# A DeltaNet and latent-attention trunk on one core: how layer A issues its small TensorE products

## The chip, the core and the metric

The kernel runs on one core of a Trainium2 chip. The time is device microseconds of one execution; three runs of the kernel before took 1349.76, 1353.17 and 1352.13, a median of 1352.13. The engines are TensorE (PE, with its weight load PEld), VectorE (DVE), ScalarE (ACT), GpSimd (POOL) and SyncE (SP), which issues the DMAs.

## The reference

A trunk of two layers over 1024 tokens of width 1024, with 16 learned meta tokens ahead of them. Layer A is a gated DeltaNet with 8 heads of 128: queries, keys and values from one projection, a causal convolution over four tokens and Silu, then the gated delta rule. Then a key and value set for latent attention is built, and layer B reads it. The change is in layer A alone:

```
qkv = silu(causal_dwconv(z[..., :2 * DN_KW + DN_VW], conv_w))
q = l2_norm(q) * (DN_DK ** -0.5);  k = l2_norm(k)
beta = sigmoid(b_raw);  g = -exp(a_log) * softplus(a_raw + dt_bias)
S_t = a_t S_{t-1} (I - b_t k_t k_t^T) + b_t v_t k_t^T,  o_t = S_t q_t      # a = exp(g)
o = rms_norm(o, o_gain) * silu(gate);  x + o @ w_out
```

The reference does the rule in chunks of tokens: inside a chunk a lower triangular system has to be solved, and a 128x128 state S goes from chunk to chunk.

## The kernel before, in words

Tokens are cut into a meta tile of 16 and eight tiles of 128. The normed input lies transposed in SBUF as two tensors hT_hi and hT_lo (reduced-precision parts that add up to the fp32 value). A projection of 128 columns is a `gemm_T` (L207) for each of three token chunks of 272, 384 and 384: 8 x 3 products called *split products* here (L91, L92, L93: high x high, high x low, low x high), accumulated in one of two "mm" banks of PSUM. ScalarE copies the result out (L370), POOL and DVE do the convolution (L372, and L375 three times), ScalarE the Silu.

The heads go in pairs. For a pair: the keys, then `key_prep` for both heads, `invert_blocks`, the values and their transposes (`natural`), the queries, `query_prep`, `finish_inverses`, and the scan over the tiles (`scan_meta`, then `scan_tile` eight times for each head). While one pair is at its inverse and scan, the projections of the next pair's keys are already issued; these split products are the work that fills PE between the small ones.

`key_prep` transposes the keys tile by tile (L397); after each, ScalarE squares the transposed tile and adds up its rows. It forms beta over the key's norm (br), which is transposed too (L416, L417), copied and written to DRAM as rows (L420, L421), makes the decay tile from two products (L431), the key products (L440) and the meta tile's (L449, L454). U goes to DRAM as 32x32 blocks (blk_in). `invert_blocks` loads these as M, 66 blocks side by side, and bb, the beta row read from DRAM (L516); after the product of the two (L519) come 31 steps of two DVE operations each (L524, L527) that hang on one another. A POOL operation (L529) follows and the store to blk_out. `finish_inverses` loads the blocks back as T64, transposes them on DVE (L554), and joins them to 64 and 128 rows with small products on PE (from L566 on, "fin" bank).

`query_prep` squares the whole of qT on ScalarE, then sums over the 128 rows of each tile with a product whose moving side is one column of ones (L475); then the products of queries and keys (L483, and L487 for the meta tile). A scan step is: S times keys (L611), r on DVE, S times queries (L615), the inverse times r (L616), u on DVE, u into the state (L621), S2 on DVE, u into the output (L625).

PSUM has two "mm" banks, three "tr", one "fin" and two "ch" for the scan. What sets the order on each engine is the scheduler of the framework: it takes the program as written and places each instruction where its model has it ready; PE, DVE, ACT, POOL and SP each run their list in that order. An instruction that waits holds up all that is behind it on its engine. After layer A's scan come the output norms (L693 on POOL), the gates, and the split of the output weights.

Of the kernel before, what the change touches and what calls it, by code (L numbers as in the profile page):

```python
# [16 lines left out]
F32 = mybir.dt.float32  # L17
# [13 lines left out]
H = 8  # L31
# [85 lines left out]
def body(ctx: ExitStack, tc: tile.TileContext, I, out):  # L117
# [64 lines left out]
    with ExitStack() as la:  # L182
# [78 lines left out]
        with ExitStack() as l0:  # L261
# [5 lines left out]
            wab2 = ap_.tile([P, KT, 2, 2 * H], F32R, tag="wab2", name="wab2", bufs=1)  # L267
            split_w(wab, wab2[:, :, 0], wab2[:, :, 1])
            abT = ap_.tile([4 * H, L], F32, tag="abT", name="abT", bufs=1)
            for c, (a, b) in enumerate(TOKC):  # L270
                ps = bank("fin", [P, 512])[0:4 * H, 0:b - a]
                for kt in range(KT):
                    w = wab2[:, kt].rearrange("p x c -> p (x c)")
                    TE.matmul(ps, w, hT_hi[:, kt, a:b], start=kt == 0, stop=False)
                    TE.matmul(ps, w, hT_lo[:, kt, a:b], start=False, stop=kt == KT - 1)
                V.tensor_copy(abT[:, a:b], ps)
            ab = ap_.tile([P, NT + 1, 2 * H], F32, tag="ab", name="ab", bufs=1)
            V.memset(ab, 0.0)
            ps = bank("tr", [P, 512])
            for t in range(-1, NT):  # L280
                a, b = tok(t)
                s = t if t >= 0 else NT
                TE.transpose(ps[0:b - a, 32 * s:32 * s + 32], abT[:, a:b], ident[:32, :32])
            for rows, s in ((slice(0, P), slice(0, NT)), (slice(0, NM), slice(NT, NT + 1))):
                p4 = ps[rows, 32 * s.start:32 * s.stop].rearrange("p (t x c) -> p t x c", x=2, c=2 * H)
                V.tensor_copy(ab[rows, s], p4[:, :, 0])
                V.tensor_tensor(out=ab[rows, s], in0=p4[:, :, 1], in1=ab[rows, s], op=ALU.add)
# [32 lines left out]
            V.tensor_tensor(out=glo, in0=g, in1=ghi, op=ALU.subtract)  # L320

# [61 lines left out]
        def key_prep(h, kn, U):  # L383

            att, kd = ([kp.tile([P, 4, P], F32, tag=y, name=nm(y), bufs=6) for _ in range(2)] for y in ("att", "kd"))
            kdm = sp.tile([NM, P], F32, tag="kdm", name=nm("kdm"), bufs=3)
# [4 lines left out]
            for half, s4 in halves() + [(2, slice(NT, NT + 1))]:  # L391
                k, tiles = (P, range(s4.start, s4.stop)) if half < 2 else (NM, (-1,))
                ps = bank("tr", [P, 4, P])
                junk = sp.tile([P, P], BF16, tag="jk", name=nm("junk"), bufs=1)
                for j, t in enumerate(tiles):
                    a, b = tok(t)
                    TE.transpose(ps[0:k, j, :], kn[:, a:b], ident)  # L397
                    act(junk[0:k], ps[0:k, j, :], AF.Square, accum_out=sk[0:k, s4.start + j, hc])
                rk4, sc4 = flat(rk[0:k, s4, hc]), sc[0:k, s4]
                rsqrt(rk4, flat(sk[0:k, s4, hc]), 1.0, EPS)  # L400
                V.tensor_tensor(out=sc4, in0=rk4, in1=flat(ekd[0:k, s4, hc]), op=ALU.mult)
                if half < 2:
                    V.tensor_tensor(out=kd[half], in0=ps, in1=sc4[:, :, None].broadcast_to([P, 4, P]),
                                    op=ALU.mult)
                else:
                    V.tensor_scalar(out=kdm, in0=ps[0:k, 0, :], scalar1=sc4, scalar2=None, op0=ALU.mult)
            for rows, s in ((slice(0, P), slice(0, NT)), (slice(0, NM), slice(NT, NT + 1))):
                x = lambda y: flat(y[rows, s, hc])
                V.tensor_tensor(out=x(br), in0=x(beta), in1=x(rk), op=ALU.mult)
                V.tensor_scalar(out=x(nbeta), in0=x(br), scalar1=-1.0, scalar2=None, op0=ALU.mult)  # L410
                if s.start == 0:
# [1058 lines left out]
```

## Time and profile before

| what | value |
|---|---|
| median of three runs | 1352.13 us (1349.76 to 1353.17) |
| the profiled execution | 1351.8 us, span 1350.1 us |
| mean granted TensorE clock | 0.989 |
| PE busy | 1306.3 us, 97% of the span |
| DVE busy | 900.1 us, 67% |
| ACT busy | 534.8 us, 40% |
| POOL busy | 412.8 us, 31% |
| last product of layer A's scan | ends at 572.8 us (572.41 + 0.43) |

The profile shows one execution. In a group's line stand source line, engine, operation, "out<-in" by the program's names, how often, then busy us and the mean ns of one, and behind the bar the idle time before them and what ended it. In a timeline stand the start, the time, the engine and the line, and in square brackets an idle time before it. A product of two fp32 operands shows as two records (x2). PE's records overlap, so the cost of one is read from the distance between starts.

### The profile page before, as it was taken

How to read it: one execution, taken by the hardware profiler on the slowest of the kernel's cores; microseconds unless marked ns; L12 is line 12 of the kernel's file. 1: busy time of each engine (PE TensorE's matmuls, PEld its weight loads, DVE VectorE, ACT ScalarE, POOL GpSimd, SP SyncE). 2: the span in 40 equal slices, each digit the busy share in tenths (PEclk: the TensorE clock that was granted, in tenths of full speed). 3: DMA queues.
4: the chain of work that ended last, by engine and by line, in shares of the span. 5: the costliest groups of instructions: out<-in, count | busy, mean ns of one | idle time of the engine just before them, and what ended most of it. 6: DMA issues, size and time to landing. Idle time of an engine off the chain costs nothing.

```text
span 1350.1 us, 24895 instructions
## 1 busy us (share of the span) xinstructions
PE 1306.3 (97%) x9064; PEld 1181.7 (88%) x9064; DVE 900.1 (67%) x2601; ACT 534.8 (40%) x1694; POOL 412.8 (31%) x680
## 2 busy tenths in 40 slices
PE   6999999999999999999999999998999999998998
PEld 4879989989998999997888798887999999998876
DVE  6669879968978884633553765224888878788221
ACT  6442343244325322211222243116777677776100
POOL 3344224323421320060101402212535435347000
PEclk9999999999999999999999999999999999999999
DMA  6111202111211113255441302311111101014443
GB/s 185 41 25 48 56 20 62 40 42 37 59 49 32 50 32 96 72 159 178 145 147 68 95 1 84 121 47 57 44 38 35 56 21 36 21 36 149 133 124 125
DMA packets 116924, 96.81 MB, mean 72 GB/s; under 512 B 28462, under 2 KB 106094, under 8 KB 116802
## 3 DMA queue, kind: packets, MB, share of 16 engines
q1 hardware_dynamic: 116802, 95.23, 23.7%
q8 instruction: 71, 1.16, 0.4%
q14 instruction: 51, 0.42, 0.1%
HBM read 68.19 MB, written 27.01 MB: 71 GB/s over the span
## 4 chain that ended last, share of the span: by engine, by line
PE 75%; DVE 8%; DMA 5%; POOL 5%; ACT 4%; issue 3%; SPq 0%; DVEq 0%; ACTq 0%; POOLq 0%
PE mm L91 7%; PE mm L93 7%; PE mm L92 7%; PE sc L93 6%; PE sc L92 6%; PE sc L91 6%; PE bd L91 3%; PE bd L93 3%; PE bd L92 3%; PE pt L1312 2%; PE tr L483 1%; DMA raw<-in_a_w_out 1%; ACT junk L82 1%; DMA out<-raw 1%; PE ch L625 1%
## 5 line engine op out<-in xcount | busy, mean ns | idle before, releaser
L91 PE MATMUL mm<-hT_hi,whi 128*128 128x384 f32 (+1 forms) x768 | 256.8, 334 | 3.5 <-DVE whi L98 3.5
L93 PE MATMUL mm<-hT_hi,wlo 128*128 128x384 f32 (+1 forms) x768 | 255.3, 332 | 0.7 <-DVE wlo L99 0.7
L92 PE MATMUL mm<-hT_lo,whi 128*128 128x384 f32 (+1 forms) x768 | 255.7, 333 | 0.0
L91 PEld LDWEIGHTS mm<-hT_hi,whi 128*128 128x128 f32 x768 | 147.4, 192 | 5.5 <-issue 4.7
L93 PEld LDWEIGHTS mm<-hT_hi,wlo 128*128 128x128 f32 x768 | 147.5, 192 | 2.5 <-DVE wlo L99 1.3
L92 PEld LDWEIGHTS mm<-hT_lo,whi 128*128 128x128 f32 x768 | 147.2, 192 | 1.4 <-issue 0.4
L108 DVE TENSOR_TENSOR pTl<-pt,pTh 128x256 fp32r<-128x256 f32 (+2 forms) x112 | 55.0, 494 | 11.0 <-ACT pTh L107 9.5
L98 POOL TENSOR_SCALAR whi<-raw 128x512 fp32r<-128x512 f32 x48 | 37.7, 799 | 70.4 <-PE mm L92 63.8
L82 ACT ACTIVATE P<-P,mx 128x144 f32<-128x144 f32 (+3 forms) x64 | 50.6, 791 | 21.8 <-DVE mx L1270 19.0
L91 PE MATMUL sc<-wo_hi,oTh 128*128 128x512 f32 (+1 forms) x144 | 57.5, 400 | 0.6 <-issue 0.6
L93 PE MATMUL sc<-wo_hi,oTl 128*128 128x512 f32 (+1 forms) x144 | 57.2, 397 | 0.0
L92 PE MATMUL sc<-wo_lo,oTh 128*128 128x512 f32 (+1 forms) x144 | 56.9, 395 | 0.0
L375 DVE SCALAR_TENSOR_TENSOR kn<-z,pcol,kn 128x384 f32<-128x384 f32 (+1 forms) x72 | 41.4, 576 | 19.4 <-POOL kn L372 18.8
L1283 POOL TENSOR_SCALAR P<-P,sl 128x144 f32<-128x144 f32 (+3 forms) x64 | 53.0, 829 | 3.7
L370 ACT COPY z<-mm 128x384 f32<-128x384 f32 (+1 forms) x72 | 31.8, 442 | 54.4 <-PE mm L93 54.3
L107 ACT CAST pTh<-pt 128x256 fp32r<-128x256 f32 (+2 forms) x112 | 47.3, 427 | 14.1 <-PE pt L1312 8.0
L99 DVE TENSOR_TENSOR wlo<-raw,whi 128x512 fp32r<-128x512 f32 x64 | 47.1, 746 | 8.5 <-POOL whi L98 8.4
L93 PE MATMUL sc<-h_hi,wlo 128*128 128x512 f32 x128 | 50.8, 397 | 0.0
L92 PE MATMUL sc<-h_lo,whi 128*128 128x512 f32 x128 | 50.6, 396 | 0.0
L91 PE MATMUL sc<-h_hi,whi 128*128 128x512 f32 x128 | 50.5, 395 | 0.0
L91 PE MATMUL bd<-wf_hi,oTh 128*128 128x512 f32 x128 | 50.2, 392 | 0.3 <-ACT oTh L1422 0.2
L102 DVE SCALAR_TENSOR_TENSOR wlo<-raw,pcol,whi 128x128 fp32r<-128x128 f32 x64 | 23.4, 429 | 40.0 <-POOL whi L101 40.0
(380 smaller groups left out, 3951.1 us busy)
## 6 DMA issues: line engine op xcount, KB each, us to landing
raw<-in_a_w_in SPq DMA_DIRECT2D x64, 256.0 KB
xt<-in_x SPq DMA_DIRECT2D x16, 512.0 KB
o_scr<-o SPq DMA_DIRECT2D x64, 64.0 KB
raw<-in_a_w_out SPq DMA_DIRECT2D x8, 512.0 KB
on<-o_scr SPq DMA_DIRECT2D x8, 512.0 KB
x_scr<-xt SPq DMA_DIRECT2D x8, 512.0 KB
raw<-in_b_w_in SPq DMA_DIRECT2D x8, 512.0 KB
gb_scr<-z SPq DMA_DIRECT2D x8, 512.0 KB
```

Source lines behind the costliest of these rows:

```text
L82: i = A.activation(out_ap, in_ap, func, **kw)
L91: TE.matmul(ps, ahi, bhi, start=first, stop=False)
L92: TE.matmul(ps, ahi, blo, start=False, stop=False)
L93: TE.matmul(ps, alo, bhi, start=False, stop=last)
L98: eng.tensor_scalar(out=hi, in0=raw, scalar1=1.0, scalar2=1.0, op0=ALU.mult, op1=ALU.mult)
L99: V.tensor_tensor(out=lo, in0=raw, in1=hi, op=ALU.subtract)
L107: A.copy(hi, ps)
L108: V.tensor_tensor(out=lo, in0=ps, in1=hi, op=ALU.subtract)
L370: A.copy(z[:, 3 + a:3 + b], gemm_T(hi, lo, c))
L375: V.scalar_tensor_tensor(out=yc, in0=z[:, a + j:b + j], scalar=col("cw", 24 * j + m), in1=yc, op0=ALU.mult, op1=ALU.add)
L1283: G.tensor_scalar(out=Pm[:, 0:n], in0=Pm[:, 0:n], scalar1=s, scalar2=1.0, op0=ALU.mult, op1=ALU.mult)
L1312: TE.transpose(pt[:, kb, x * P:(x + 1) * P], Ps[x][0][:, y0 + kb * P:y0 + (kb + 1) * P], ident)
```

## The change

Eight edits, all in layer A.

1. `query_prep`: the one-column products go. The query tiles are transposed (four, four and one, each group in a "tr" bank), and ScalarE squares each transposed tile from PSUM and adds up its rows.
2. `key_prep`: the key transposes are issued four in a row, then the four squares; the meta tile is handled as 128 rows.
3. `key_prep`: br is no longer transposed. SP writes it to DRAM straight from its columns, in pieces of four bytes.
4. The meta tile's products run over 128 rows: the decay product, the key and query products, the inverse times values and the state product. For that the meta rows of beta and ekd beyond 16 are zero, and the inverse tiles Nm are four fixed tiles that are cleared once.
5. `natural` transposes the meta tile as 128 columns.
6. `scan_meta` and `scan_tile`: products that don't need a DVE result are issued ahead of it.
7. The columns of the b and a projection are padded to 128 with zeros; their transposes go in groups over three banks.
8. epsq comes from one DVE operation instead of two.

The diff, cut to its core ("..." is left out):

```diff
@@ key_prep
-            kdm = sp.tile([NM, P], F32, tag="kdm", name=nm("kdm"), bufs=3)
+            kdm = sp.tile([P, P], F32, tag="kdm", name=nm("kdm"), bufs=3)
...
-                for j, t in enumerate(tiles):
-                    a, b = tok(t)
-                    TE.transpose(ps[0:k, j, :], kn[:, a:b], ident)
-                    act(junk[0:k], ps[0:k, j, :], AF.Square, accum_out=sk[0:k, s4.start + j, hc])
+                for j in range(n):
+                    a = tok(s4.start + j)[0] if half < 2 else 0
+                    TE.transpose(ps[:, j, :], kn[:, a:a + P], ident)
+                for j in range(n):
+                    act(junk, ps[:, j, :], AF.Square, accum_out=sk[:, s4.start + j, hc])
...
-            TE.transpose(ps[0:NT, 0:P], flat(br[:, 0:NT, hc]), ident)
-            TE.transpose(ps[0:1, P:P + NM], br[:NM, NT, hc], ident[:NM, :NM])
-            V.tensor_copy(brow, ps[0:NT, 0:P])
-            V.tensor_copy(browm, ps[0:1, P:P + NM])
-            SY.dma_start(beta_scr[h, NM:].rearrange("(t p) -> t p", p=P), brow)
-            SY.dma_start(beta_scr[hc, 0:NM], browm)
+            SY.dma_start(beta_scr[h, NM:].rearrange("(t p) -> p t", p=P), flat(br[:, 0:NT, hc]))
+            SY.dma_start(beta_scr[h, 0:NM], br[:NM, NT, hc])
...
-            TE.matmul(ps[:NM, 0:NM], after[:NM, :NM], gmm, start=True, stop=True)
+            TE.matmul(ps[:, 0:NM], after, gmm, start=True, stop=True)
...
-            TE.matmul(ps[:NM, 0:NM], kn[:, 0:NM], kn[:, 0:NM], start=True, stop=True)
+            TE.matmul(ps[:, 0:NM], kn[:, 0:P], kn[:, 0:NM], start=True, stop=True)
@@ query_prep
-            for a, b in TOKC:
-                act(sq[:, a:b], qT[:, a:b], AF.Square)
-            for t in range(-1, NT):
-                a, b = tok(t)
-                s = t if t >= 0 else NT
-                TE.matmul(ps[0:b - a, s:s + 1], sq[:, a:b], one, start=True, stop=True)
...
+            for s4 in (slice(0, 4), slice(4, 8), slice(NT, NT + 1)):
+                ps = bank("tr", [P, 4, P])
+                junk = sp.tile([P, P], BF16, tag="jk", name=nm("junk"), bufs=1)
+                for j in range(s4.stop - s4.start):
+                    a = tok(s4.start + j)[0] if s4.start < NT else 0
+                    TE.transpose(ps[:, j, :], qT[:, a:a + P], ident)
+                for j in range(s4.stop - s4.start):
+                    act(junk, ps[:, j, :], AF.Square, accum_out=qss[:, s4.start + j:s4.start + j + 1])
+            V.tensor_scalar(out=epsq[:, :, h], in0=qss, scalar1=EPS * P, scalar2=EPS * EPS * P, op0=ALU.mult,
+                            op1=ALU.add)
...
-            TE.matmul(ps[:NM, 0:NM], kn[:, 0:NM], qT[:, 0:NM], start=True, stop=True)
+            TE.matmul(ps[:, 0:NM], kn[:, 0:P], qT[:, 0:NM], start=True, stop=True)
@@ scan_meta, scan_tile
-            TE.matmul(ps[:NM, 0:P], c["Nm"], c["vbm"], start=True, stop=True)
-            A.copy(u, ps[:NM, 0:P])
+            TE.matmul(ps[:, 0:P], c["Nm"], c["vbm"], start=True, stop=True)
+            A.copy(u, ps[:, 0:P])
             TE.matmul(ps[:, P:2 * P], c["kdm"], u, start=True, stop=True)
+            TE.matmul(ps[:NM, 2 * P:3 * P], c["attm"], u, start=True, stop=True)
...
             TE.matmul(ps[:, 0:P], c["kn"][:, a:b], S, start=True, stop=True)
+            TE.matmul(ps[:, 2 * P:3 * P], c["qT"][:, a:b], S, start=True, stop=True)
...
-            TE.matmul(ps[:, 2 * P:3 * P], c["qT"][:, a:b], S, start=True, stop=True)
             TE.matmul(ps[:, P:2 * P], c["N"][:, t, :], r, start=True, stop=True)
...
                 TE.matmul(ps[:, 0:P], c["kd"][t // 4][:, t % 4, :], u, start=True, stop=True)
+            TE.matmul(ps[:, 3 * P:4 * P], c["att"][t // 4][:, t % 4, :], u, start=True, stop=True)
+            if t < NT - 1:
...
-            TE.matmul(ps[:, 3 * P:4 * P], c["att"][t // 4][:, t % 4, :], u, start=True, stop=True)
...
+        Nms = [[bp.tile([P, P], F32, name=f"Nm{i}{hl}") for hl in range(2)] for i in range(2)]
+        for x in Nms[0] + Nms[1]:
+            G.memset(x, 0.0)
```

How the order on PE moves at three places. First, `query_prep` of the first pair's second head (tr are "tr" banks, sq the squares, kn the keys; mm is a projection). Before:

```order
L93 MATMUL mm_252_1667<-hT_hi,wlo_231_1456 128x384
L475 MATMUL tr_263_1846<-ones,sq_262_1845 16x1
L475 MATMUL tr_263_1846<-ones,sq_262_1845 128x1 x8
L483 MATMUL tr_264_1861<-qT_235_1466,kn_103_657 128x128 x4
L483 MATMUL tr_265_1867<-qT_235_1466,kn_103_657 128x128 x4
L487 MATMUL tr_266_1873<-qT_235_1466,kn_103_657 16x16
L91 MATMUL mm_273_1889<-hT_hi,whi_244_1592 128x272
```

After the change:

```order
L93 MATMUL mm_253_1676<-hT_hi,wlo_227_1455 128x384
L471 MATMUL tr_262_1853<-ident,qT_231_1465 128x128 x4
L471 MATMUL tr_264_1863<-ident,qT_231_1465 128x128 x4
L471 MATMUL tr_266_1873<-ident,qT_231_1465 128x128
L91 MATMUL mm_277_1906<-hT_hi,whi_245_1601 128x272
L92 MATMUL mm_277_1906<-hT_lo,whi_245_1601 128x272
```

Nine one-column products and the nine products behind them stood in a row; now nine transposes stand there, and the products of queries and keys (L480, L484) come in three parts after eight, four and no further split products.

Second, the start of the first pair's `finish_inverses` (fin, L566, now L561), with the next pair's keys. Before:

```order
L93 MATMUL mm_472_2654<-hT_hi,wlo_268_1877 128x272
L91 MATMUL mm_472_2654<-hT_hi,whi_267_1876 128x272
L397 MATMUL tr_392_2319<-ident,kn_249_1603 128x128
L92 MATMUL mm_472_2654<-hT_lo,whi_267_1876 128x272
L566 MATMUL fin_258_1720<-T_0_253_1698,U_107_752 32x32 x32
L397 MATMUL tr_392_2319<-ident,kn_249_1603 128x128
L93 MATMUL mm_472_2654<-hT_hi,wlo_268_1877 128x272
```

After the change:

```order
L92 MATMUL mm_278_1937<-hT_lo,whi_245_1601 128x384
L93 MATMUL mm_278_1937<-hT_hi,wlo_246_1602 128x384
L91 MATMUL mm_279_1968<-hT_hi,whi_245_1601 128x384
L561 MATMUL fin_257_1727<-T_0_254_1707,U_109_769 32x32 x32
L92 MATMUL mm_279_1968<-hT_lo,whi_245_1601 128x384
L93 MATMUL mm_279_1968<-hT_hi,wlo_246_1602 128x384
```

The first inverse product stood inside the first chunk (272 columns, mm_472) of the keys of the next pair's second head; it now stands at the start of the third chunk (384 columns, mm_279) of the first head's keys, so 23 split products of that chunk and those of mm_472 now come behind it.

Third, the next pair's key transposes (L397, now L404) at the same stretch, of which the rows of before above show two, alone between split products. After the change:

```order
L93 MATMUL mm_279_1968<-hT_hi,wlo_246_1602 128x384
L591 MATMUL ch_280_1999<-vbm_201_1221,Nm_539 128x128
L591 MATMUL ch_285_2012<-vbm_224_1450,Nm_540 128x128
L404 MATMUL tr_391_2314<-ident,kn_250_1612 128x128 x4
L404 MATMUL tr_396_2336<-ident,kn_250_1612 128x128
L576 MATMUL fin_259_1814<-T_0_254_1707,U_109_769 64x64 x16
L593 MATMUL ch_280_1999<-um_281_2000,kdm_114_774 128x128
L594 MATMUL ch_280_1999<-um_281_2000,attm_143_883 16x128
L593 MATMUL ch_285_2012<-um_286_2013,kdm_152_903 128x128
L594 MATMUL ch_285_2012<-um_286_2013,attm_181_1011 16x128
L404 MATMUL tr_396_2336<-ident,kn_250_1612 128x128 x3
L404 MATMUL tr_401_2357<-ident,kn_250_1612 128x128
L91 MATMUL mm_470_2653<-hT_hi,whi_271_1893 128x272
```

Four and then further transposes stand in a row, together with the meta tile's inverse and state products (L591, L593, L594), which stood alone too.

104 lines of the change are left out of this document (48 added, 56 removed).

## The prediction, made before the changed kernel ran

> **What bounds the kernel now.** I read the page first (busy times and the chain that ended last), then the busy time by stage, then the clock, then single stretches of TensorE's timeline.
>
> ```profile
> PE 1306.3 (97%) x9064; PEld 1181.7 (88%) x9064; DVE 900.1 (67%) x2601; ACT 534.8 (40%) x1694; POOL 412.8 (31%) x680
> PE 75%; DVE 8%; DMA 5%; POOL 5%; ACT 4%; issue 3%; SPq 0%; DVEq 0%; ACTq 0%; POOLq 0%
> ```
>
> PE is busy for 97% of the span and carries 75% of the chain, so time that leaves PE should leave the kernel, unless another engine is right behind it. The averages hide that one is. The busy time by stage (columns: stretch, its length, then busy us and count of PE, PEld, DVE, ACT, POOL; granted clock; DMA share; GB/s) for the four inversion stretches, one per head pair, and the gate stage:
>
> ```profile
> 100.00:150.00 50.00, 50.00 (x330) 49.01 (x329) 48.44 (x115) 12.31 (x28) 18.14 (x26) 0.97 0.17 44
> 215.00:270.00 55.00, 55.00 (x367) 53.67 (x366) 53.37 (x138) 14.18 (x37) 23.17 (x26) 0.97 0.21 55
> 335.00:390.00 55.00, 54.84 (x358) 53.36 (x357) 50.56 (x133) 14.30 (x38) 20.28 (x24) 0.95 0.21 54
> 456.00:511.00 55.00, 54.18 (x358) 52.96 (x357) 48.23 (x133) 12.73 (x35) 15.69 (x14) 0.97 0.19 50
> 573.00:629.00 56.00, 51.79 (x313) 50.52 (x311) 21.71 (x34) 6.65 (x17) 23.79 (x16) 0.97 0.46 142
> ```
>
> While a pair's blocks are inverted, PE and DVE are both full: DVE 88 to 97%. The inverse is a chain on DVE, and PE ends its part of the pair with the products that need it. For the second pair the timeline shows the chain from the last key product to the first inverse product:
>
> ```profile
> 203.60 0.61 PE L440 MATMUL tr<-kn 128*128 128x128 f32 x4
> 214.94 0.32 SPq L513 DMA_DIRECT2D M<-blk_in  x1
> 268.87 0.17 DVE L527 TENSOR_TENSOR M<-M,tmp 66x31 f32<-66x31 f32 x1
> 278.62 1.43 DVE L554 STREAM_TRANSPOSE U<-T 32x512 f32<-32x512 f32 x2
> 279.91 0.58 PEld L566 LDWEIGHTS fin<-T,U 32*32 32x32 f32 x32 [0.16 <-issue]
> ```
>
> The first of the two transposes that PE needs ends about 279.3 (half of 1.43 after 278.62), 0.6 us before PE starts. So the chain has next to no slack: if PE comes earlier, it waits.
>
> **Part 1: query norms.** Per head, nine one-column products (L475, 18 records) become nine transposes (L471); epsq takes one DVE operation instead of two, and three squares of 384 columns become nine of 128. From the chain in order of time, and PE's timeline ahead of the first block:
>
> ```profile
> 126.07 0.34 PE L93 MATMUL mm<-hT_hi,wlo 128*128 128x384 f32 x1
> 126.34 2.08 PE L475 MATMUL tr<-ones,sq 128*16 128x1 f32 x18
> 126.41 2.01 PE tr L475 x18
> 143.76 2.01 PE tr L475 x18
> 355.20 0.87 PE tr L497 x8
> ```
>
> Eight transposes of the same shape took 0.87 us, nine take 9/8 x 0.87 = 0.98. A split product of 384 columns starts 0.176 us after the last one, so entering the block cost 126.34 - 126.07 - 0.176 = 0.09. Saved: 8 heads x (2.01 + 0.09 - 0.98) = **-9.0 us** on PE. ScalarE's part:
>
> ```profile
> L82 ACT ACTIVATE junk<-tr 128x128 bf16<-128x128 f32 (+1 forms) x18 | 5.0, 276 | 6.1 <-PE tr L397 5.9
> L82 ACT ACTIVATION_READ_ACCUMULATOR junk<-tr 128x1 f32 (+1 forms) x18 | 3.5, 194 | 0.0
> ```
>
> Nine squares at 0.276 + 0.194 are 4.2 us a head. ACT is busy for 12 to 15 of the 50 to 55 us of an inversion stretch, which hides it; uncovered it would be at most 4.2 us a head, less the three squares that go. The banks: nine transposes fill three "tr" banks, and the products behind them need one back after four squares, 1.9 us; the order puts eight split products (1.0 us) in between in the first pair, so up to 1 us a head could come back as a wait. That bound, +8, goes into the range.
>
> **The clock.** The busy time of windows of 3.41 us, with PE's granted clock in the column before the last two: the first slowed one and the last of five in the query stage, the window ahead of the first, and one that was not slowed:
>
> ```profile
> 124.97:128.38 3.41, 3.41 (x28) 3.14 (x27) 2.92 (x7) 0.43 (x1) 3.02 (x3) 1.00 0.24 69
> 128.38:131.79 3.41, 3.41 (x17) 3.29 (x16) 3.34 (x10) 1.63 (x4) 0.68 (x1) 0.50 0.00 0
> 145.45:148.86 3.41, 3.41 (x30) 3.25 (x31) 3.36 (x11) 0.00 (x0) 0.14 (x1) 1.00 0.20 50
> 500.43:503.84 3.41, 3.41 (x19) 3.19 (x17) 0.97 (x2) 0.20 (x1) 0.00 (x0) 0.50 0.00 0
> ```
>
> Five such windows ran at half clock between 128.38 and 503.84, each right after a window that held nearly all of an L475 block (126.41 to 128.38: 1.97 us). The block at 143.76 had at most 1.69 us in one window, up to 145.45, and the next window ran at 1.00. So a window with about 2 us of one-column work slows the next, one with 1.7 does not. The transposes last 0.98 us, below both. Taken: 5 x 3.41 / 2 = **-8.5 us**; bounds -8.5 and +5.1 (all eight heads slowed, the rule below).
>
> The Trainium skill ("TensorE: Matmul & The Clock Gate", Part 4: PE-mode transpose) says of transposes that the clock gate "doesn't count" them as busy the same way. By that rule a run of nine would be idle for the gate as the one-column products seem to be. By that rule the clock's term would be +5.1 (three windows more, 3 x 1.71) instead of -8.5. No trace here holds nine transposes in a row; the row at 143.76 speaks against the loss even if they don't count, since 0.98 is under 1.69.
>
> **Part 2: key transposes.** PE issued them singly, each behind ScalarE's square of the one before:
>
> ```profile
> 281.57 0.29 PE L93 MATMUL mm<-hT_hi,wlo 128*128 128x272 f32 x1
> 281.83 0.33 PE L397 MATMUL tr<-ident,kn 128*128 128x128 f32 x1
> 281.91 0.37 PE L91 MATMUL mm<-hT_hi,whi 128*128 128x272 f32 x1
> 282.12 0.28 PE L92 MATMUL mm<-hT_lo,whi 128*128 128x272 f32 x1
> 282.24 0.29 PE L93 MATMUL mm<-hT_hi,wlo 128*128 128x272 f32 x1
>   ACT junk L82: 7.0, 29
> ```
>
> The last row is from the waits of this line: PE or its weight load sat idle 29 times. From 281.57 to 282.12 are 0.55 us; two split products of 272 columns are 0.25 (282.12 to 282.24 is one), so the lone transpose costs 0.30, against 0.11 in a group. 29 x 0.19 = 5.5; some wait stays with the first of a group. Taken **-4.5**, bounds -5.5 and +3.
>
> **Part 3: 128 rows instead of 16.**
>
> ```profile
> 204.50 0.39 PE L616 MATMUL ch<-r,U 128*128 128x128 f32 x2
> 204.81 0.21 PE L449 MATMUL tr<-gmm,after 16*16 16x16 f32 x2
> 205.18 0.29 PE L92 MATMUL mm<-hT_lo,whi 128*128 128x272 f32 x1
> 287.77 0.33 PE L93 MATMUL mm<-hT_hi,wlo 128*128 128x384 f32 x1
> 288.03 0.39 PE L595 MATMUL ch<-vbm,Nm 16*16 16x128 f32 x2
> 288.62 0.34 PE L92 MATMUL mm<-hT_lo,whi 128*128 128x384 f32 x1
> ```
>
> A full fp32 product is two records of 0.112, 0.224 us (204.50 and the next start, 204.72). Taking the split products around them off, L449 cost 205.18 - 0.126 - 204.72 = 0.33 and L595 288.62 - 287.77 - 2 x 0.176 = 0.50. So 0.11 and 0.28 go when they are full height. L454 and L487 are taken as L449, L597 as between (0.15), and the two beta transposes L416/L417 as 0.41 (they leave with two copies): 3 x 0.11 + 0.28 + 0.15 + 0.41 = 1.17 a head, **-9.4 us**; bounds -12 and -5, by taking all as the one or the other. L600 keeps 16 output rows.
>
> **Part 4: the scan's order.** L608 now stands ahead of r, and L618 ahead of the next state. Both stay on PE. DVE's r and S2 then wait for one product more of their own head, 0.224 each; between them PE has the other head's products. Taken 0; bounds -3 and +7 (one product for each of 8 steps x 4 pairs = 7.2, if nothing covers it).
>
> **Part 5: beta written in 4-byte pieces** (L417), 1024 packets a head, and SP's next entry, the load of bb (before: L516), waits for them; behind it stand blk_in's stores and M's load (before: L513).
>
> ```profile
> q1 hardware_dynamic: 56304, 23.79, 17.9%
> L516 SPq DMA_DIRECT2D bb<-beta_scr x8: 302/307/414, 76.3 to 444.3; - x8
> L513 SPq DMA_DIRECT2D M<-blk_in x4: 300/312/354, 100.8 to 456.3; - x4
> ```
>
> The first row is DMA from 40 to 560 us (packets, MB, share of 16 engines): a packet took 0.179 x 16 x 520 / 56304 = 0.0265 us of one engine. 1024 of them are 1.7 us spread over 16 engines, 27 us on one. In the last pair bb's load was issued 12 us ahead of M's (444.3 and 456.3), in the first 24. Taken 0 by the spread; if all went to one engine, some 15 us late in a pair.
>
> **The sum on PE** is -9.0 - 8.5 - 4.5 - 9.4 = -31.4. Two things come on top. The order moves 36 split products (of 1998) from ahead of the scan's last product to behind it: 36 x 0.17 = 6 us that the gate stage must take in. Its row has 56.00 - 51.79 = 4.2 us of idle PE, and the chain there is not PE's:
>
> ```profile
> 571.33 3.44 DMA raw<-in_a_w_out
> 576.36 11.36 POOL ro L693 x7
> ```
>
> So I charge 3 of the 6: net -3.
>
> **What comes next: the inverse.** Ahead of the first inverse product PE now has less to do, over the four pairs: 53 split products fewer (53 x 0.17 = 9.0; for the second pair the order shows 342 and 325), 47 scan products fewer (x 0.224 = 10.5), the query norms (9.0), the clock (8.5), and of parts 2 and 3 what stands there (14 lone transposes, 2.7; 16-row products, 2.4). Together 42 us earlier. DVE's chain gets shorter too, because 54 fewer DVE operations stand between its first and its last step (counted in the order, -7, -13, -22, -12 by pair): at 53.37 / 138 = 0.39 us, 21 us, and up to 1 us of slack a pair makes 25. So PE would stand **42 - 25 = 17 us** more at L561: +17. Bounds: 0, if the chain follows in full, and 42, if it does not shorten. DVE at 97% in the row of 215 to 270 puts the value at the DVE count.
>
> -31.4 - 3 + 17 = -17.4. The profiled execution took 1351.8 (span 1350.1, 1.7 around it); 1351.8 - 17.4 = 1334.4, and the median is 0.3 above that execution: **about 1334.5 us**.
>
> **Rivals.** Under about 4 us (0.3%) a change cannot be told from none here.
>
> (a) *The chain follows PE.* The order puts the inverse earlier, and DVE has fewer operations in front. If the added wait is 0 to 10, the time is 1317.5 to 1327.5; say 1323. Against it: next to no slack in the second pair. 0.22.
>
> (b) *The transposes slow the clock like the one-column products.* Then eight windows, 13.7 us, are slow where I have none. All eight lie ahead of an inverse where I expect PE to wait 4 us a pair, so most of it replaces waiting: 1335 to 1348, say 1340. The row at 143.76 speaks against it. 0.08. (The rule of the Trainium skill in "TensorE: Matmul & The Clock Gate", Part 4: PE-mode transpose, would have it this way.)
>
> (c) *Slower: the inverse does not come earlier at all.* Place: L561 in each pair; price 42 instead of 17, so -31.4 - 3 + 42 = +7.6, 1359.7. It decides from an added wait of 34, where the change is worth nothing; DVE would have to save none of its 21 us. DVE's fullness speaks for it, the shorter order against. 0.06.
>
> (d) *Slower: beta's store blocks SP's queue* by 27 us a head. Some 15 us later in each pair, 4 x 15 - 17 = +43, 1395; it decides from about 4 us a pair. 0.04.
>
> (e) *The change does nothing that lasts*: parts of (c) and of the bank bound, 1348 to 1356. 0.06.
>
> **Numbers.** Forecast 0.54, an added wait of 11 to 24: 1328 to 1341. With (a) below and (b) and a part of (e) above, 8 in 10 lie within **1318 to 1349**. Faster by over 0.3%: forecast, (a), (b) and little else, 0.85; within: (e) and the edge of (c), 0.07; slower: (d) and most of (c), 0.08.
>
> **What would show it.** In the profile after: L471 at 0.98 us for nine, no half-clock window behind it; L404 with no waits on ScalarE's squares; no 16-row product over 0.25. PE idle at the first inverse product, released by DVE, 3 to 6 us a pair, with DVE still over 90% busy ahead of it; the scan's end 20 us earlier (572.8 now), the gate stage 3 us longer. It is wrong if PE stays full up to L561 (then (a)), if half-clock windows follow L471 (b), or if the inverse starts as late after the last key product as now (c), with SP waiting behind L417 (d).

## The result, and the profile after

The changed kernel took 1366.27 us (median of four runs, 1361.66 to 1368.5) against 1351.83 of the kernel before: a ratio of 1.0104, 95% interval 1.0072 to 1.0135. It is slower by 14 us, where I had forecast 17 us faster, and lies above the range that I gave (1318 to 1349).

The profiled execution took 1364.6 us, span 1362.9. The page's busy times and the chain that ended last:

```profile
PE 1291.3 (95%) x8976; PEld 1182.8 (87%) x8976; DVE 898.6 (66%) x2565; ACT 548.6 (40%) x1814; POOL 415.9 (31%) x686
PE 65%; DVE 13%; DMA 8%; POOL 6%; ACT 5%; issue 3%; SPq 0%; DVEq 0%; POOLq 0%; ACTq 0%
```

PE is busy for 15 us less than before, as it should be, and the span is 13 us longer: PE stands idle for 28 us more. On the chain, PE's share falls from 75% to 65%, and DVE and DMA take it over. So the work did go, and waits came in its place. The stages, from the starts and ends of the lines in both traces (us):

| milestone | before | after | step before | step after |
|---|---|---|---|---|
| last key product, pair 1 | 95.2 | 90.4 | | |
| first inverse product, pair 1 | 163.5 | 159.2 | 68.3 | 68.8 |
| last key product, pair 2 | 204.2 | 203.5 | 40.7 | 44.3 |
| first inverse product, pair 2 | 279.9 | 277.9 | 75.7 | 74.4 |
| last key product, pair 3 | 325.0 | 332.6 | 45.1 | 54.7 |
| first inverse product, pair 3 | 404.1 | 408.0 | 79.1 | 75.4 |
| last key product, pair 4 | 447.1 | 457.4 | 43.0 | 49.4 |
| first inverse product, pair 4 | 521.2 | 532.7 | 74.1 | 75.3 |
| end of layer A's scan | 572.8 | 581.5 | 51.6 | 48.8 |
| end of the span | 1350.1 | 1362.9 | 777.3 | 781.4 |

From the last key product to the first inverse product, where by my count 42 us of PE's work would leave, the four pairs together take 293.9 us instead of 297.2. PE is busy for 27 us less in these steps (269.1 us, before 296.2) and for 10 us more in the others up to the scan's end (269.0, before 258.8), which together got 12 us longer. So nearly all of the 27 us came back as waits. What fills the first kind of step shows in the waits of layer A (60 to 640 us; what waited, for what, us in total, times, longest), of PE, of DVE and, to 580 us, of SP:

```profile
PE tr L480 <- ACT junk L82: 14.2, 7, 4.0
DVE o L624 <- DMA o_scr<-o: 11.6, 4, 4.0
DVE M L516 <- DMA M<-blk_in: 3.9, 1, 3.9
SPq L513 <- DMA beta_scr<-br: 34.9, 5, 9.9
```

In the kernel before the first two don't occur, the third has 0.2 us, and the answer to the fourth is

```profile
SPq L516 <- DMA beta_scr<-brow: 2.6, 5, 0.6
```

The first and the last begin a story each.

**The banks.** The timeline of the first pair's query preparation:

```profile
128.21 1.14 PE L471 MATMUL tr<-ident,qT 128*128 128x128 f32 x9
129.03 0.43 ACT L82 ACTIVATE qT<-qT 128x272 f32<-128x272 f32 x1 [4.78 <-DVE qT L382]
131.63 0.52 ACT L82 ACTIVATE qT<-qT 128x384 f32<-128x384 f32 x1 [2.16 <-DVE qT L382]
132.42 0.28 ACT L82 ACTIVATE junk<-tr 128x128 bf16<-128x128 f32 x1
134.02 0.28 ACT L82 ACTIVATE junk<-tr 128x128 bf16<-128x128 f32 x1
134.04 1.22 PE L480 MATMUL tr<-qT,kn 128*128 128x128 f32 x4 [3.67 <-ACT junk L82]
```

The nine transposes end at 129.35 and fill three "tr" banks. The first square starts at 132.42, because in ScalarE's list two Silu operations of the next projection stand ahead of it, and the second of these waits until 131.63 for DVE, which is busy with the inverse. The four squares of the first bank end at 134.02, and PE's next product needs that bank: it stood still for 3.67 us. ScalarE is busy for a quarter of this stretch (11.85 of the 42 us from 108 to 150); what made it late is its order, not its load. Nearly all of the 14.2 us are four such waits of 2.8 to 4.0 us, one in the first head of each pair; the other three are of 0.16 to 0.26 us.

**The clock behind such a wait.** Windows of 3.41 us again (PE's busy time is the second figure, the granted clock the third from the end):

```profile
130.42:133.83 3.41, 0.00 (x0) 0.00 (x0) 3.34 (x7) 2.11 (x10) 3.41 (x3) 1.00 0.00 0
133.83:137.24 3.41, 3.20 (x15) 3.21 (x15) 3.00 (x8) 2.14 (x13) 0.94 (x2) 0.50 0.31 79
253.30:256.71 3.41, 0.67 (x6) 0.45 (x4) 3.34 (x7) 1.92 (x9) 3.41 (x3) 1.00 0.00 0
256.71:260.12 3.41, 3.01 (x14) 3.01 (x15) 3.00 (x8) 2.32 (x13) 1.01 (x2) 0.50 0.31 77
342.05:345.46 3.41, 0.66 (x4) 0.34 (x2) 2.75 (x7) 0.40 (x2) 0.00 (x0) 1.00 0.39 78
345.46:348.87 3.41, 2.82 (x10) 2.82 (x11) 3.25 (x7) 0.52 (x1) 0.59 (x2) 0.50 0.65 164
```

A window in which PE was busy for 0 to 0.67 us is followed by one at half clock. Between 60 and 640 us there are eight windows at half clock now, where before there were six. Six of the eight stand behind the four long waits for squares: one each from 133.83 and 256.71, two in a row each from 383.00 and 509.29. The other two, from 345.46 and 468.34, stand behind waits that come from the store (next). A window at half clock costs at most half of its 3.41 us, so a wait of 3 to 4 us costs up to 1.7 us once more, or 3.4 where two windows follow.

**The store.** SP's and DVE's timelines around the second pair's second beta store, and the packets in the 2.4 us from 200.4 on (40 slices of 0.06 us; tenths of 16 DMA engines):

```profile
200.08 0.39 SPq L417 DMA_DIRECT2D beta_scr<-br  x1
200.52 0.57 SPq L418 DMA_DIRECT2D beta_scr<-br  x1
211.08 0.32 SPq L513 DMA_DIRECT2D bb<-beta_scr  x1
```

```profile
DMA  0269952000598777777850000000000000000000
```

```profile
213.47 0.35 DVE L624 TENSOR_SCALAR o<-ch,egc 128x128 f32<-128x128 f32 x1 [3.65 <-DMA o_scr<-o]
```

```profile
214.13 0.49 PE L612 MATMUL ch<-r,U 128*128 128x128 f32 x2 [3.27 <-DVE r L610]
```

The store's packets (the second hill) are through at about 201.7, after some 0.7 us, spread over the engines at 70 to 80%. My estimate was 1.7 us. But the load of bb, which waits for the store, was issued at 211.08: for 9 us no packet of the store moved that the trace shows, and SP stood (9.9 us by its waits). Behind it stood the scan's output stores. DVE has three buffers for these, and stopped at 209.8 for 3.65 us; the scan's r was behind it, and PE stopped too. The load of M went out at 217.49, 14.0 us after the pair's last key product; before, it was at 214.94, 10.7 us after it.

### The profile page after: what moved, and what is told of

It reads as the page before. It is cut to its first block, busy times and chain, and to the rows that moved or that the text cites. A ratio compares the mean times of both kernels' runs of the same rounds, so it can differ in the third digit from the quotient of the medians.

```text
span 1362.9 us, 24811 instructions
## 1 busy us (share of the span) xinstructions
PE 1291.3 (95%) x8976; PEld 1182.8 (87%) x8976; DVE 898.6 (66%) x2565; ACT 548.6 (40%) x1814; POOL 415.9 (31%) x686
## 4 chain that ended last, share of the span: by engine, by line
PE 65%; DVE 13%; DMA 8%; POOL 6%; ACT 5%; issue 3%; SPq 0%; DVEq 0%; POOLq 0%; ACTq 0%
PE sc L93 6%; PE sc L92 6%; PE sc L91 6%; PE mm L93 5%; PE mm L91 5%; PE mm L92 5%; PE bd L91 4%; PE bd L93 4%; PE bd L92 4%; DMA o_scr<-o 2%; DVE qT L382 2%; ACT junk L82 2%; PE pt L1313 2%; PE tr L480 2%; DVE M L524 1%
## 5 line engine op out<-in xcount | busy, mean ns | idle before, releaser
L92 PE MATMUL mm<-hT_lo,whi 128*128 128x384 f32 (+1 forms) x768 | 252.9, 329 | 0.0
L108 DVE TENSOR_TENSOR pTl<-pt,pTh 128x256 fp32r<-128x256 f32 (+2 forms) x112 | 54.9, 494 | 10.7 <-ACT pTh L107 9.2
L107 ACT CAST pTh<-pt 128x256 fp32r<-128x256 f32 (+2 forms) x112 | 47.2, 426 | 14.2 <-PE pt L1313 7.2
L1282 POOL TENSOR_SCALAR Pe<-P,sl 128x128 f32<-128x128 f32 x64 | 28.3, 444 | 71.3 <-DVE sl L1279 52.1
```

Of the source, the lines that this page charges most:

```text
L92: TE.matmul(ps, ahi, blo, start=False, stop=False)
L107: A.copy(hi, ps)
L108: V.tensor_tensor(out=lo, in0=ps, in1=hi, op=ALU.subtract)
L1282: G.tensor_scalar(out=Pe, in0=Pm[:, None, 0:NM].broadcast_to([P, E8, NM]), scalar1=s, scalar2=1.0, op0=ALU.mult, op1=ALU.mult)
```

## The experiments

The kernels below differ by the edit shown. Ratios are to the kernel before, timed beside it.

**1. Beta as rows again**

```diff
-            SY.dma_start(beta_scr[h, NM:].rearrange("(t p) -> p t", p=P), flat(br[:, 0:NT, hc]))
-            SY.dma_start(beta_scr[h, 0:NM], br[:NM, NT, hc])
+            TE.transpose(ps[0:NT, 0:P], flat(br[:, 0:NT, hc]), ident)
+            TE.transpose(ps[0:1, P:P + NM], br[:NM, NT, hc], ident[:NM, :NM])
+            ...
+            SY.dma_start(beta_scr[h, NM:].rearrange("(t p) -> t p", p=P), brow)
```

> The changed kernel, with beta again transposed on TensorE, copied and stored to DRAM as rows (the old path); all else as changed. Theory S (SyncE's queue): in the changed kernel SP stands some 10 us behind each beta store (issues at 200.52 and 211.08 us of the profile), so the output stores come late, VectorE waits 11.6 us for their buffers and the inverse of each pair starts some 3 us later. With rows the stand goes to about 1 us, VectorE's waits for the output buffers go to 0, from the last key product to the inverse's first step falls from 17 to 20 us per pair to 15 to 17, and the time falls by about 13, from 1366 to 1353. Theory B (banks and clock in the query preparation: TensorE waits 14.2 us for ScalarE's squares, and eight windows at half clock cost 13.7 us): the store matters little, 1363 or more, and those waits stay.

Measured: 1355.85 us, ratio 1.0034 (1.0015 to 1.0054); 10 less than the changed kernel. DVE no longer waits for output buffers. PE's wait for the squares is what it was:

```profile
PE tr L487 <- ACT junk L82: 14.6, 7, 3.6
```

So the store costs about 10 us here (theory S), and the second loss is untouched (theory B). Neither theory alone was right.

**2. Query norms by one-column products again**

```diff
-            for s4 in (slice(0, 4), slice(4, 8), slice(NT, NT + 1)):
-                ...
-                    TE.transpose(ps[:, j, :], qT[:, a:a + P], ident)
+                act(sq[:, a:b], qT[:, a:b], AF.Square)
+            ...
+                TE.matmul(ps[0:b - a, s:s + 1], sq[:, a:b], one, start=True, stop=True)
```

> The changed kernel, with the query norms again from three large squares and one-column products; all else as changed (beta in 4-byte pieces too). Theory B: TensorE's 14.2 us of waits for the squares and the eight half-clock windows go, the old five windows (8.5 us) and the old products (9 us) come back: 14.2 + 13.7 - 8.5 - 9 = 10 less, 1356. Theory S: SP's stand behind the beta store stays and with it the late inverse, so that TensorE only waits at the inverse instead: 1361 to 1368.

Measured: 1348.15 us, ratio 0.9981 (0.9959 to 1.0002), 18 less than the changed kernel and more than theory B's 10. SP and DVE still wait for the store, which costs less here:

```profile
SPq L513 <- DMA beta_scr<-br: 52.7, 8, 8.8
DVE o L624 <- DMA o_scr<-o: 3.3, 3, 2.3
DVE M L516 <- DMA M<-blk_in: 7.0, 2, 4.1
```

SP stands longer than before the edit (52.7 against 34.9 us), DVE's waits behind it are 10.3 against 15.5. So the length of SP's stand alone does not say what it costs; what is queued behind it counts.

**3. and 4. One part alone, in the kernel before**

The first of the two kernels takes the diff of experiment 1 in reverse, the second that of experiment 2.

> The kernel before with one edit alone: beta is written to DRAM straight from its columns, in 4-byte pieces, and its two transposes and copies go. Theory S: SP stands about 10 us behind each of the eight stores, and the kernel gets slower by about 10 to 13 us, 1362 to 1365, although TensorE has 3 us less to do. Theory B: no slower than before, 1348 to 1352.

> The kernel before with one edit alone: query norms from nine transposes in three banks and nine squares on ScalarE. Theory B: TensorE waits for a bank behind the squares, about 14 us in all, and half-clock windows follow these waits (up to 13.7 us against 8.5); with 9 us saved on products that is 14 + 5 - 9 = +10, 1362. Theory S: the edit saves what I predicted for it or nothing, 1340 to 1352.

Measured: beta in pieces alone 1359.26 us, ratio 1.0053 (1.0029 to 1.0077), +7. Query transposes alone 1364.7 us, ratio 1.0090 (1.0062 to 1.0118), +12. Their waits, of SP in the first and of PE in the second:

```profile
SPq L509 <- DMA beta_scr<-br: 44.3, 8, 8.1
```

```profile
PE tr L483 <- ACT junk L82: 13.3, 7, 3.8
```

Each of the two parts makes the kernel before slower by itself. Both theories hold, each for its part; for the first the figure is below the 10 to 13 expected.

**5. Both undone**

> The changed kernel with two parts undone: beta goes through transposes and rows again, and the query norms through one-column products. What stays is the grouped key transposes, the 128-row meta products and the scan's order. If the two undone parts are the whole loss and simply add (-10 and -18 in the runs with one undone), about 1338, 13 under the kernel before. If the inverse on VectorE then bounds each pair (the prediction's part on what comes next), TensorE waits at the first inverse product and 1344 to 1350.

Measured: 1341.49 us, ratio 0.9924 (0.9896 to 0.9951). This beats both kernels, by 10 and by 25 us, and lies between my two cases. PE's waits at the inverse are 1.0 us, those for ScalarE's squares are gone, and the others are single ones of at most 1.4 us. The two undone parts add up nearly: 10 + 18 = 28 singly, 25 together.

**6. Rows, and the query transposes in the scan's banks**

```diff
-                ps = bank("tr", [P, 4, P])
+                ps = bank("ch" if s4.start < NT else "tr", [P, 4, P])
```

> The changed kernel with beta through rows again, and the query transposes kept but written to the two scan banks (ch), which nothing else uses at that time; only the meta tile's goes to a tr bank. If the loss of the query part was the wait for a bank behind late squares, TensorE's waits for ScalarE's squares go from 14 to under 3 us and the half-clock windows of the query stage go with them: 1325 to 1340. If the transposes themselves slow the clock, half-clock windows stay behind them: 1340 to 1350. If the squares being late on ScalarE is what costs, no change against the run with rows alone, 1353 to 1358.

Measured: 1350.31 us, ratio 0.9991 (0.9978 to 1.0004); 5.5 less than with rows alone. The wait did not go. It moved on:

```profile
PE tr L491 <- ACT junk L82: 12.5, 5, 4.0
PE ch L478 <- ACT junk L82: 2.2, 2, 1.6
```

The meta tile's transpose still took one of three "tr" banks, its square is the last of nine on ScalarE, and the third product group behind it (L491) needs that bank. The experiment did not separate what it was made for; number 9 does.

**7. As 5, with the scan step in its old order**

```diff
-            TE.matmul(ps[:, 2 * P:3 * P], c["qT"][:, a:b], S, start=True, stop=True)
             r = ...
+            TE.matmul(ps[:, 2 * P:3 * P], c["qT"][:, a:b], S, start=True, stop=True)
             ...
-            TE.matmul(ps[:, 3 * P:4 * P], c["att"][t // 4][:, t % 4, :], u, start=True, stop=True)
             S2 = ...
+            TE.matmul(ps[:, 3 * P:4 * P], c["att"][t // 4][:, t % 4, :], u, start=True, stop=True)
```

> As the run with both parts undone, and the scan step (not the meta step) in its old order too. I took 0 for the new order, with bounds -3 and +7. If the longer chain of products in one step counts, this is up to 7 us faster than the run with both undone; if the order helps, it is up to 3 us slower.

Measured: 1348.44 us, ratio 0.9981 (0.9960 to 1.0002): the new order is worth 7 us in this company, on the other side of my bounds.

**8. Five output buffers in the changed kernel**

```diff
-            o = sp.tile([P, P], F32, tag="o", name=nm("o"), bufs=3)
+            o = sp.tile([P, P], F32, tag="o", name=nm("o"), bufs=5)
```

> The changed kernel with five buffers instead of three for the scan's output tile; all else as changed, beta in 4-byte pieces too. SP still stands 10 us behind each beta store. If VectorE's wait for the output buffers (11.6 us in all) is how that stand costs time, it falls to under 3 us and the time falls by 5 to 10, to about 1358. If the late blocks (the inverse's start) are how it costs, the time stays within 3 us of 1366.

Measured: 1361.0 us, ratio 1.0067 (1.0043 to 1.0090), 5 less. DVE's wait for the buffers is gone, and much of it has turned into the other one, the wait for M:

```profile
DVE M L516 <- DMA M<-blk_in: 14.6, 4, 5.3
SPq L513 <- DMA beta_scr<-br: 39.7, 6, 9.0
```

So SP's stand reaches DVE by two ways, and freeing one leaves the other.

**9. No bank held by late squares**

Beta by rows, the eight tiles' transposes in the two scan banks, and the meta tile's norm as a single one-column product that shares the bank of its query-key product.

```diff
+            act(sqm, qT[:, 0:NM], AF.Square)
+            for s4 in (slice(0, 4), slice(4, 8)):
+                ps = bank("ch", [P, 4, P])
...
             TE.matmul(ps[:, 0:NM], kn[:, 0:P], qT[:, 0:NM], start=True, stop=True)
+            TE.matmul(ps[:NM, 32:33], sqm, one, start=True, stop=True)
```

> The changed kernel with beta through rows again, the query transposes of the eight tiles in the two scan banks, and the meta tile's norm (16 tokens) by one one-column product in the bank of its query-key product, so that no product of the query preparation waits for a bank that late squares hold. In the run with scan banks the wait had only moved to the meta product (12.5 us). If that wait and the half-clock windows it leads to are the loss of the query part, both vanish: TensorE's waits for the squares under 2 us, no half-clock window right behind the transposes, and 1333 to 1341, at or under the run with both parts undone (1341). If the transposes themselves slow the clock, the windows stay, 1341 to 1348.

Measured: 1347.91 us, ratio 0.9968 (0.9954 to 0.9983), above the 1333 to 1341 that I expected. Its windows at the first pair's query preparation (transposes from 126.86 on), and at the inverse, and PE's two largest waits in layer A:

```profile
126.98:130.40 3.42, 3.42 (x33) 3.37 (x32) 3.33 (x6) 0.20 (x1) 1.53 (x3) 1.00 0.00 0
130.40:133.81 3.41, 3.41 (x27) 3.41 (x27) 2.94 (x8) 3.19 (x17) 1.53 (x1) 1.00 0.19 44
157.80:161.21 3.41, 0.55 (x34) 0.55 (x36) 3.34 (x5) 1.01 (x4) 1.33 (x3) 1.00 0.36 57
161.21:164.62 3.41, 3.41 (x53) 3.35 (x47) 3.13 (x6) 2.79 (x17) 0.60 (x1) 0.50 0.42 98
```

```profile
PE fin L573 <- DMA T<-blk_out: 9.1, 3, 3.8
PE ch L480 <- ACT junk L82: 3.0, 1, 3.0
```

Behind these transposes the clock stays at 1.00. The one wait for squares is in the last pair: the transposes of its second head waited 3.02 us, until 493.51, for a scan bank that the first head's squares still held, and two windows at half clock follow:

```profile
488.89:492.30 3.41, 1.60 (x16) 1.48 (x15) 3.41 (x8) 0.97 (x5) 1.49 (x1) 1.00 0.00 0
492.30:495.71 3.41, 2.20 (x10) 2.20 (x11) 3.41 (x9) 3.22 (x17) 0.00 (x0) 0.50 0.00 0
```

From 60 us on, all other windows at half clock in layer A of this kernel stand behind the waits at the inverse. The changed kernel shows the same for nine transposes. In the first pair's second head they start at 148.11, the wait behind them is 0.16 us, and the clock stays:

```profile
147.49:150.90 3.41, 3.25 (x26) 3.00 (x25) 3.21 (x9) 2.91 (x13) 2.13 (x3) 1.00 0.00 0
150.90:154.31 3.41, 3.41 (x30) 3.25 (x29) 2.89 (x4) 1.37 (x8) 1.72 (x2) 1.00 0.67 168
```

So eight or nine transposes do not slow the clock, and the windows at half clock in the changed kernel came from PE's waits. But with PE free in the query stage, it now waits for the inverse, 9.1 us in three pairs, and a half-clock window follows each time. That is the wait I had predicted for the changed kernel, in its place, at half the size that I gave it (17 us). What the transposes save on PE (9.0 by part 1) is about what it loses there, so that this kernel is no faster than number 5, whose query part keeps the one-column products. Number 5 is even faster, by some 6 us (1341.49 and 1347.91, by ratio 0.9924 and 0.9968); most of that is the clock of the executions, to which I come below.

**10. to 12. The other parts**

Number 10 is number 5 with the key transposes issued singly; 11 is the kernel before with the scan step's new order alone; 12 is number 5 with both of these undone.

```diff
-                for j in range(n):
                     TE.transpose(ps[:, j, :], kn[:, a:a + P], ident)
-                for j in range(n):
                     act(junk, ps[:, j, :], AF.Square, accum_out=sk[:, s4.start + j, hc])
```

> As the run with both parts undone (1341), but the key transposes issued singly again, each with its square. I put the grouping at -4.5 us: so 1346. If the time they stood alone was hidden, 1341 to 1343.

> The kernel before with the new order of the scan step alone. Undone in the changed kernel's better version it cost 7 us (1341 to 1348). If the order itself is worth that (fewer hand-offs between TensorE and VectorE in a step), 1344 to 1347; if it only pays together with the other parts, or that difference came from how the scheduler laid out the rest, 1350 to 1354.

> The changed kernel with four parts undone: beta through rows, one-column query norms, single key transposes, the old order of the scan step. What stays is the 128-row meta products, the padded b and a projection and the single epsq operation. I put the 128-row products at -9.4 us (the two beta transposes, 0.41 a head, stay here: -6): 1346. If the stretches where they stand are bounded by VectorE and not TensorE, 1350 to 1353. With it the parts alone can be added: this, the scan's order alone (-5.6) and the grouping (the run with both undone against the one with single keys, -5).

Measured: 10: 1346.88, ratio 0.9960 (0.9943 to 0.9976). 11: 1346.55, 0.9956 (0.9937 to 0.9976). 12: 1348.78, 0.9978 (0.9956 to 0.9999). In number 10 the single transposes have their waits back, in number 5 the line has none; of number 10, PE and its weight load ahead of L404:

```profile
  ACT junk L82: 7.3, 30
```

So beside the other two parts grouping the keys is worth 5 us. The scan's order alone is worth 6, and the 128-row products (with the padded b and a projection) 3, at the edge of what can be told from none. (Number 12 has the two epsq operations of before, and not the single one that its expectation names; so have all kernels with one-column norms.) The parts do not add: 128 rows with the scan's order (number 10) is no better than the scan's order alone, 128 rows with grouping (number 7) no better than 128 rows alone, and all three together give 10. In each kernel the scheduler lays out the split products anew, so a difference of two kernels holds that too.

**The clock of the executions.** A profile shows the windows of one execution, but the mean granted clock of each execution is on record. (1 - clock) x span is the time that it would cost if PE bounded the whole kernel:

| kernel | median us | lost clock, mean us | executions |
|---|---|---|---|
| before | 1351.1 to 1352.1 | 15.0 | 81 |
| changed | 1366.27 | 20.5 | 4 |
| 1, beta as rows | 1355.85 | 16.9 | 10 |
| 2, one-column norms | 1348.15 | 14.7 | 10 |
| 3, beta in pieces alone | 1359.26 | 21.1 | 10 |
| 4, query transposes alone | 1364.7 | 24.5 | 8 |
| 5, both undone | 1341.49 | 10.1 | 4 |
| 6, transposes in scan banks | 1350.31 | 15.2 | 10 |
| 7, as 5, old scan order | 1348.44 | 16.6 | 10 |
| 8, five output buffers | 1361.0 | 20.4 | 4 |
| 9, no bank held | 1347.91 | 17.9 | 10 |
| 10, as 5, single keys | 1346.88 | 13.4 | 7 |
| 11, scan order alone | 1346.55 | 12.6 | 8 |
| 12, 128 rows | 1348.78 | 13.6 | 10 |

Among executions of one kernel, 1 us of lost clock went with 0.65 us of time (my estimate: a straight line through 182 executions of the kernel before and of numbers 1 to 12). By this the clock makes 5 of the 6 us between numbers 5 and 9, 4 of the 7 between 5 and 7, and 4 of the 7 that beta in pieces costs alone. At one clock, 0.990, two executions of number 5 took 1343.03 and 1344.78, and three of number 9 1344.5, 1346.14 and 1348.72. Why two of number 5's four executions had 0.993 and 0.997 no trace shows. So a difference of 3 to 7 us between two of these kernels is only in part the work that was moved.

## Why the prediction was wrong, step by step

**Part 1, query norms and bank wait (-9.0, bound +8): the step that failed first.** The transposes cost about what I said: nine from 128.21 to the start of the next product at 129.11, 0.90 us, where I had 0.98. The bank wait I put at up to 1 us a head, "after four squares, 1.9 us": I counted from the moment of the transposes, as if ScalarE were free. Its share of busy time said so, and the share was the wrong view. ScalarE runs its list in order, and the list has a Silu ahead that waits for DVE. PE waited 14.2 us, nearly all of it in the first head of each pair (experiments 2, 4 and 9 show it from both sides). The part alone made the kernel before 12 us slower.

**The clock (-8.5): mechanism half right, size and sign wrong.** The five windows did belong to the one-column products. The rule that I took from them holds in all fourteen traces here, counted from 60 to 560 us in the windows of 3.41 us: of 23 windows with 2.0 us or more of one-column products 22 were followed by half clock, of 42 with 1.0 to 1.95 us none. Nor do nine transposes slow the clock (against rival b; experiment 9). Whether they count as work for it stays open, since their 0.90 us are fewer than the 1.95 us of one-column products that slowed nothing. But I had not asked what a PE that waits does to the clock. In the same traces each of 22 windows with under 1.35 us of PE work was followed by half clock, and the changed kernel had eight slowed windows between 60 and 640 us. The trace of before held one slowed window behind such a wait, which I passed over since it lies in the gate stage (PE busy for 1.78 us in the window from 599.42, half clock from 602.83). The Trainium skill ("TensorE: Matmul & The Clock Gate", What's actually happening) describes a free-running window of 3413 ns after which an idle engine runs at half clock; these rows agree with it (3.41 us, 0.00 busy, then 0.50). Here a window need not be wholly idle (1.32 us of work from 505.88 in the changed kernel, then 0.50).

**Part 5, the store (0): wrong, by the step from the packets to the landing.** The packets took less than I estimated, 0.7 us and not 1.7, spread over the engines. What SP waits for is the end of the store, and for that I had no term: bb's load was issued 5.6 to 10.0 us behind the store in the eight heads. I also misread the room ahead of M's load. The 24 us in the first pair are those of its first head's bb; the second head's stood 8 us ahead (92.7 and 100.8). My rival (d) had the place and the way (SP's queue, the late loads) with 27 us a head from all packets on one engine; its time was added up wrongly, since 43 us above the forecast are 1377 and not 1395. It was 5 to 10 us of stand, and by number 8 about half of its cost went through the output buffers, which I had not named. Alone it cost 7 us, in the changed kernel 10.

**What comes next, the inverse (+17): right in its place, but covered.** In the changed kernel PE does not wait at L561, since it loses the same time earlier, in the query stage (14.2 us and the clock), and since the chain itself starts later. From the last key product to M's load (starts 102.47, 217.49, 345.60 and 471.13) the four pairs take 52.8 us together; before (100.82, 214.94, 335.56 and 456.27) it was 36.1, and with beta as rows in number 1 it is 34.5. From M's load to the first inverse product they take 241.2 us instead of 261.1. So this part did get 20 us shorter, near the 21 to 25 that I had for the chain, and the store's stand took 17 of them back. (It ends with PE's arrival, so the chain itself may have been shorter still.) In experiment 9, where neither loss is left, PE waits 9.1 us there. Rival (c), that the stretch up to the inverse does not get shorter, is what the table shows (3 us of 42), but by another way than (c)'s: DVE did have less to do (592 operations instead of 652 in these steps).

**Part 2 (-4.5):** right beside the new scan order: 5 us between numbers 10 and 5, and the waits on ScalarE's squares are gone from the line. Without that order it brought nothing (numbers 12 and 7, 1348.78 and 1348.44).

**Part 3 (-9.4):** half right. PE's timeline in the changed kernel, where L451 stands alone between split products:

```profile
205.10 0.33 PE L93 MATMUL mm<-hT_hi,wlo 128*128 128x384 f32 x1
205.27 0.33 PE L451 MATMUL tr<-kn 128*128 128x16 f32 x2
205.45 0.42 PE L91 MATMUL mm<-hT_hi,whi 128*128 128x384 f32 x1
205.71 0.38 PE L612 MATMUL ch<-r,U 128*128 128x128 f32 x2
```

From 205.10 to 205.71 are 0.61 us; less two split products of 0.176 the full product costs 0.26, not the 0.224 I took and not the 0.33 or more of 16 rows. Alone the part gave 3 us (number 12), where 6 were left of my 9.4 with the beta transposes kept.

**Part 4 (0, bounds -3 to +7):** mis-sized; 6 us faster alone, 7 in number 5. The longer chain that I had priced is there: DVE's waits for PE ahead of r and S2 (60 to 640 us) rise from 10.6 to 19.4 us in number 11. The kernel got faster all the same. That PE and DVE hand over less often, as I expected for number 11, the traces do not show: DVE waits for scan products 63 times, 27.5 us in all, against 56 times and 23.8 us before. Part of the gain is the clock (12.6 us lost instead of 15.0); what brings the rest stays open.

**The gate stage (+3):** 777.3 to 781.4, +4.1.

In sum: the parts that I put at -4.5, -9.4 and 0 gave -10 together (number 5; of the -9.4, 3.3 are the beta transposes, which number 5 keeps). That this is close to my -10.6 for what number 5 has is in part luck, since some 3 of the 10 us are its clock (10.1 us lost instead of 15.0). The two that I put at -17.5 (query norms and their clock) and 0 (the store) gave +25: the wait for a bank behind late squares, the clock behind that wait, and the end of the store are the three things that the sum lacked.

## What to carry to other kernels

Before a product's input is moved to another engine, ask what stands ahead of it in that engine's list and what that waits for; a busy share of a quarter says nothing about when the result is there, and a PSUM bank is held until it is. When a store is cut into small pieces, price its end and not its packets, and look at all that is queued behind the first instruction that waits for it. And a wait of some 3 us on TensorE costs more than itself, since the next window may run at half clock.

## What had not been expected of the hardware

The store of 4 KB in 4-byte pieces: its packets moved in some 0.7 us, spread over the engines, and the load that waits for it went out 5.6 to 10.0 us behind the store; as rows of 512 bytes, SP waited 0.6 us at most in the kernel before and 0.7 in number 1 for the same data. What happens in between no trace here shows.

And the granted clock: a window of 3.41 us with little PE work (under 1.35 us, 22 of 22), or with 2 us of one-column products (22 of 23), was followed by a window at half clock, while a window with 0.9 us of transposes and otherwise full of products was not. The kernels here differ by it (10.1 to 24.5 us of lost clock in the mean), and so do the executions of one kernel, each us of it with some 0.65 us of time.
